# Half of nine weight splits per layer moved from GpSimd to VectorE, and one addition of squares moved into PSUM

## The chip, the core and the metric

The kernel runs on one core of a Trainium2 chip. The metric is the device time of one execution in microseconds. Five engines work side by side, each through a queue of its own in a fixed order: TensorE (PE in the profile, with its weight loads as PEld), VectorE (DVE), ScalarE (ACT), GpSimd (POOL) and SyncE (SP), which here issues nearly all transfers.

## What is computed

Two layers of a hybrid trunk over 640 tokens (512 latent, 128 context), model width 1024. Cut to what matters here:

```python
def trunk_layer(x, cvec, lw, layer, ctx):
    sh1, sc1, g1, sh2, sc2, g2 = modulation(cvec, lw['w_mod'], lw['b_mod'])
    h = rmsnorm(x, lw['g_mix']) * (1.0 + sc1) + sh1
    mixed, new_ctx = token_mixers(h, lw, layer, ctx)   # h @ w_in -> DA | MLA | NA | conv -> @ w_out
    x = x + g1 * mixed
    h = rmsnorm(x, lw['g_ff']) * (1.0 + sc2) + sh2
    x = x + g2 * (jnp.square(jax.nn.relu(h @ lw['w_ff1'])) @ lw['w_ff2'])
    return x, new_ctx
```

The columns of `h @ w_in` feed four groups: differential attention (DA), latent attention (MLA), neighbourhood attention (NA) and a convolution of 31 taps over 256 channels (conv). In MLA the low rank vectors are normalised first: `qm = heads(rmsnorm(mla_qd, lw['g_mla_q']) @ lw['w_mla_qup'], MLA_HEADS)`, where `mla_qd` has 256 columns.

## The kernel before

**Products from split numbers.** A large product is made of three matmuls (`mm3`, L245 to L247): each operand is split into a rounded high part and the rest, and high x high, high x low and low x high are summed in PSUM. Weights come in *granules* of 128 x 1024 floats, 94 per layer, in the order in which they are used. Granule n of the program (layer 1 begins at 94) is loaded into one of three raw buffers (`w_dma`, L215, on SP's queue), then split by `w_cut` in two halves of 512 columns: for each half ScalarE casts the high part (L193) and another engine subtracts to get the low part (L194). That engine is GpSimd, but for some halves that the condition in `w_cut` gives to VectorE. Of granules 4 to 29 of a layer ("mix" granules) the high and low parts alternate between two slots, so granule n can only be cast when TensorE is done with granule n-2, and the raw buffer of n takes granule n+3 when both halves are split.

**What granules 4 to 12 are.** 0 to 3 are the conv columns; 4 and 5 the NA values, 6 to 9 NA queries and keys (eight steps of 128 rows each, the second half of the granule being steps 4 to 7); 10 to 12 the DA values and the rotary key of MLA (three, three and two steps of 288 columns); 13 is the first of the DA queries, 14 of its keys.

**What else runs there.** When the conv columns are done, `conv_taps` puts 62 VectorE instructions on a background list (L420 and L424, two times 31 taps over 670 columns). They are traced with a lower priority than the work around them (`later`), and `conv_finish` begins with an addition of the two halves on GpSimd (L439) that needs the last of them. In layer 0 the modulation of that layer is computed in the same stretch (`mod_rows`): groups of four 512 KB tiles of `w_mod` are loaded by SP (L1363) into a ring of six, multiplied by TensorE (L1375), copied by ScalarE (L1382), gathered by TensorE (L1385) and added to the bias by VectorE (L1386).

**What sets the order.** The kernel's text gives each instruction a place and a priority; the framework's scheduler then fixes, when the program is built, the order of every engine's queue, by priority among what its own estimate of the times holds ready. On the chip a queue is not reordered: an instruction that waits holds all behind it.

**The low rank norm.** `lora_norm` (L630 to L646) squares each of its sources on ScalarE (L635), adds the two squares on GpSimd where there are two (L638), lets three steps of the surrounding work pass, sums over partitions by a matmul with a matrix of ones (L642), takes the inverse root (L338, L339) and scales. With two sources it is called twice per layer, for 384 and for 256 tokens; its three calls per layer for the key-value part have one source.

Of the kernel before, what the change touches and what calls it, by code (L numbers as in the profile page):

```python
# [12 lines left out]
ALU = mybir.AluOpType  # L13
# [18 lines left out]
NGRAN, NMIX = 94, 30  # L32
# [28 lines left out]
CUT = "DDDDDGDD"  # L61
# [22 lines left out]
class Builder:  # L84
# [133 lines left out]
    def w_cut(self):  # L218
        while self.w_split < min(self.w_load, self.ng):
            n = self.w_split  # L220
            i = self.w_slot(n)
            if self.held[i] or (i > 1 and self.we is None):
                return
            self.held[i] = True
            raw = self.w_raw(n)
            hi, lo = self.w_hl(n)
            for j, s in enumerate((slice(0, 512), slice(512, 1024))):
                self.split(hi[:, s], lo[:, s], raw[:, s], self.nc.vector if n < 4 and CUT[n * 2 + j] == "D" or n > 3 and j and i > 1 and n % NGRAN < NMIX + 4 else None)
            self.w_split += 1
            self.w_dma()  # L230

# [397 lines left out]
    def lora_norm(self, srcs, gains, scale):  # L629
        nc = self.nc  # L630
        n = srcs[0].shape[1]
        sqs = []
        for s in srcs:
            sq = self.tmp(n)
            nc.scalar.activation(sq, s, AF.Square)  # L635
            sqs.append(sq)
        if len(sqs) > 1:
            nc.gpsimd.tensor_tensor(out=sqs[0], in0=sqs[0], in1=sqs[1], op=ALU.add)  # L638
        for _ in range(3):
            yield  # L640
        ps = self.g()[:, 0:n]
        nc.tensor.matmul(ps, self.ones, sqs[0], start=True, stop=True)  # L642
        r = self.tmp(n)
        self.rsq(r, ps, scale)
        for s, g in zip(srcs, gains):
            nc.vector.scalar_tensor_tensor(out=s, in0=s, scalar=g, in1=r, op0=ALU.mult, op1=ALU.mult)  # L646
# [1067 lines left out]
```

## Time and profile before

| | us |
|---|---|
| median of 3 runs | 1711.4 (1711.36 to 1712.46) |
| profiled execution, its own time | 1712.74 |
| its span, first to last instruction | 1710.7 |
| TensorE busy | 1633.3 (95%) |
| VectorE busy | 1051.2 (61%) |
| ScalarE busy | 728.2 (43%) |
| GpSimd busy | 659.3 (39%) |

TensorE is nearly always at work, so its idle stretches, and the stretches in which its clock is granted at half, are what can be had. The waits are therefore read first, then the stretch around each of the long ones. All times inside the trace count from the first instruction.

### The profile page before, as it was taken

The page shows a single profiled execution, that of the slowest core. Times are in us where ns is not written, and L with a number is a line of the kernel's source. Part 1 is how long each engine was busy: PE and PEld are TensorE (multiplying, and loading weights), DVE is VectorE, ACT ScalarE, POOL GpSimd, SP SyncE. Part 2 cuts the span into 40 slices and gives each one's busy share as a digit, 9 for nine tenths or more (in the row PEclk, how much of TensorE's full clock was granted, in tenths as well). Part 3 has the DMA queues.
Part 4 walks back from the last instruction along what each step waited for, and adds up shares of the span by engine and source line. Part 5 has one row for each costly group of instructions (what it writes and reads, how often), then busy time and mean ns, then how long its engine had stood idle before and what let it go on. Part 6 is the DMA issues. An engine that isn't in the chain of part 4 may idle for free. (4 is left out here: it accounts for less than half of the span.)

```text
span 1710.7 us, 29286 instructions
## 1 busy us (share of the span) xinstructions
PE 1633.3 (95%) x11416; PEld 1531.2 (90%) x11416; DVE 1051.2 (61%) x2064; ACT 728.2 (43%) x1617; POOL 659.3 (39%) x527
## 2 busy tenths in 40 slices
PE   7989999999899999999999899999999999999997
PEld 4867988878899999999999888887789999999997
DVE  4791438867788787885377943886773333333335
ACT  4322576755622222233343257676553323332222
POOL 0242543414444444544324364341443333333330
PEclk7998999999999999999999999999999999999999
DMA  9465333302244454443222233330112222222221
GB/s 358 157 227 173 100 101 98 88 21 79 71 151 157 151 159 152 157 150 99 75 71 72 65 95 101 86 87 21 50 57 92 74 75 75 75 74 75 75 62 62
DMA packets 62330, 178.27 MB, mean 104 GB/s; under 512 B 8656, under 2 KB 20048, under 8 KB 62192
## 3 DMA queue, kind: packets, MB, share of 16 engines
q1 hardware_dynamic: 61984, 176.14, 33.7%
q8 instruction: 89, 1.46, 0.4%
q14 instruction: 49, 0.40, 0.1%
q0 software_dynamic: 64, 0.14, 0.0%
q10 hardware_dynamic: 144, 0.13, 0.0%
HBM read 158.52 MB, written 3.83 MB: 95 GB/s over the span
## 5 line engine op out<-in xcount | busy, mean ns | idle before, releaser
L194 POOL TENSOR_TENSOR ra<-fa,ra 128x512 fp32r<-128x512 f32 (+1 forms) x239 | 353.4, 1494 | 501.8 <-ACT ra L193 481.9
L194 POOL TENSOR_TENSOR we<-fa,we 128x512 fp32r<-128x512 f32 x126 | 185.7, 1485 | 261.3 <-ACT we L193 239.6
L1098 DVE TENSOR_TENSOR fr<-fr 128x384 f32<-128x384 f32 (+1 forms) x128 | 102.2, 800 | 281.5 <-ACT or L1097 153.5
L193 ACT CAST ra<-fa 128x512 fp32r<-128x512 f32 (+1 forms) x240 | 147.2, 622 | 252.7 <-PE s L246 152.7
L245 PE MATMUL s<-ra 128*128 128x256 f32 (+2 forms) x704 | 218.7, 311 | 2.4 <-DVE fa L1386 2.1
L246 PE MATMUL s<-ra 128*128 128x256 f32 (+2 forms) x704 | 217.8, 309 | 0.0
L247 PE MATMUL s<-ra 128*128 128x256 f32 (+2 forms) x704 | 217.4, 309 | 0.0
L393 DVE SCALAR_TENSOR_TENSOR fa<-s,fa 128x128 f32<-128x128 f32 (+1 forms) x312 | 121.9, 427 | 73.8 <-PE s L247 73.7
L193 ACT CAST we<-fa 128x512 fp32r<-128x512 f32 x132 | 81.5, 620 | 180.5 <-PE s L246 132.2
L302 DVE CUSTOM_DVE_ANT_0 fa<-fa 128x1024 f32<-128x1024 f32 x96 | 153.4, 1598 | 0.1
L245 PEld LDWEIGHTS s<-ra 128*128 128x128 f32 x704 | 134.2, 191 | 8.4 <-issue 4.0
L393 DVE SCALAR_TENSOR_TENSOR fa<-g,fa 128x128 f32<-128x128 f32 (+1 forms) x264 | 109.2, 443 | 44.5 <-PE g L247 43.8
L246 PEld LDWEIGHTS s<-ra 128*128 128x128 f32 x704 | 134.1, 190 | 2.4 <-issue 2.3
L247 PEld LDWEIGHTS s<-ra 128*128 128x128 f32 x704 | 134.0, 190 | 0.2 <-issue 0.2
L247 PE MATMUL g<-ra 128*128 128x256 f32 (+2 forms) x404 | 123.7, 306 | 9.1 <-POOL ra L194 9.1
L245 PE MATMUL g<-ra 128*128 128x256 f32 (+2 forms) x404 | 128.1, 317 | 0.7 <-ACT fa L656 0.4
L424 DVE SCALAR_TENSOR_TENSOR fa<-fa 128x670 f32<-128x670 f32 x120 | 127.0, 1123 | 0.4
L246 PE MATMUL g<-ra 128*128 128x256 f32 (+2 forms) x404 | 123.4, 306 | 0.0
L245 PE MATMUL g<-or,ra 128*128 128x384 f32 (+1 forms) x328 | 112.8, 344 | 4.8 <-DVE or L194 4.4
L246 PE MATMUL s<-ra,we 128*128 128x256 f32 (+1 forms) x360 | 112.2, 312 | 4.6 <-DVE ra L371 4.6
L245 PE MATMUL s<-ra,we 128*128 128x256 f32 (+1 forms) x360 | 110.6, 309 | 4.2 <-DVE fa L393 2.3
L247 PE MATMUL s<-ra,we 128*128 128x256 f32 (+1 forms) x360 | 110.5, 307 | 0.0
(294 smaller groups left out, 4425.1 us busy)
## 6 DMA issues: line engine op xcount, KB each, us to landing
fa<-in_wg SPq DMA_DIRECT2D x187, 512.0 KB, 3.7
fa<-in_wmod SPq DMA_DIRECT2D x68, 512.0 KB, 4.3
at<-in_wmod SPq DMA_DIRECT2D x25, 512.0 KB, 7.2
ra<-ra SPq DMA_DIRECT2D x64, 96.0 KB, 2.5
ra<-ra SPq DMA_DIRECT2D x64, 80.0 KB, 2.8
fa<-in_nab SPq DMA_DIRECT2D x24, 192.0 KB, 4.0
fa<-in_xT SPq DMA_DIRECT2D x8, 320.0 KB, 6.7
os<-in_wmod SPq DMA_DIRECT2D x3, 512.0 KB, 10.2
```

The source lines that it names most:

```text
L193: nc.scalar.copy(hi, src)
L194: (lo_eng or nc.gpsimd).tensor_tensor(out=lo, in0=src, in1=hi.bitcast(F32), op=ALU.subtract)
L245: nc.tensor.matmul(out, a[0], b[0], start=start, stop=False)
L246: nc.tensor.matmul(out, a[0], b[1], start=False, stop=False)
L247: nc.tensor.matmul(out, a[1], b[0], start=False, stop=stop)
L302: self.nc.vector.tensor_tensor_reduce(out=self.junk, in0=slot, in1=self.cb[:, v], scale=1.0, scalar=0.0, op0=ALU.mult, op1=ALU.add, accum_ ...
L393: self.mark = nc.vector.scalar_tensor_tensor(out=xs, in0=ps[:, a - t0:b - t0], scalar=self.mod(l, v, which)[:, m:m + 1], in1=xs, op0=ALU.m ...
L424: nc.vector.scalar_tensor_tensor(out=y, in0=g[:, j:j + 670], scalar=dwh[:, c, j:j + 1], in1=y, op0=ALU.mult, op1=ALU.add)
L1098: nc.vector.tensor_tensor(out=r, in0=r, in1=r, op=ALU.mult)
```

## The change

In `w_cut`, the second half (`j` is 1) of granules 4 to 12 of both layers is subtracted by VectorE instead of GpSimd; the first half stays on GpSimd. That is 18 instructions, 9 per layer. In `lora_norm`, the addition of the two squares on GpSimd is gone; the matmul with ones is done once per source and sums in PSUM, which makes one matmul more in each of the two calls per layer that have two sources.

```diff
-                self.split(hi[:, s], lo[:, s], raw[:, s], self.nc.vector if n < 4 and CUT[n * 2 + j] == "D" or n > 3 and j and i > 1 and n % NGRAN < NMIX + 4 else None)
+                self.split(hi[:, s], lo[:, s], raw[:, s], self.nc.vector if n < 4 and CUT[n * 2 + j] == "D" or n > 3 and j and (i > 1 and n % NGRAN < NMIX + 4 or 4 <= n % NGRAN < 13) else None)
```

```diff
             sqs.append(sq)
-        if len(sqs) > 1:
-            nc.gpsimd.tensor_tensor(out=sqs[0], in0=sqs[0], in1=sqs[1], op=ALU.add)
         for _ in range(3):
             yield
         ps = self.g()[:, 0:n]
-        nc.tensor.matmul(ps, self.ones, sqs[0], start=True, stop=True)
+        for sq in sqs:
+            nc.tensor.matmul(ps, self.ones, sq, start=sq is sqs[0], stop=sq is sqs[-1])
```

## Rows read from the trace of the kernel before

**Rows 1.** The page, busy time of engines: us, share, instructions.
```profile
PE 1633.3 (95%) x11416; PEld 1531.2 (90%) x11416; DVE 1051.2 (61%) x2064; ACT 728.2 (43%) x1617; POOL 659.3 (39%) x527
```
**Rows 2.** Waits of PE: engine, line, waited for: us in total, times, longest.
```profile
PE g L247 <- POOL ra L194: 9.1, 1, 9.1
PE s L1375 <- DMA at<-in_wmod: 5.8, 2, 4.4
...
PE s L245 <- DVE fa L1386: 2.1, 1, 2.1
...
PE g L642 <- POOL fa L638: 1.2, 2, 0.6
```
**Rows 3.** Timeline of PE, layer 1: start, length, instruction, idle before and releaser.
```profile
976.50 0.34 PE L246 MATMUL g<-ra 128*128 128x384 f32 x1
985.98 0.69 PE L247 MATMUL g<-ra 128*128 128x384 f32 x1 [9.14 <-POOL ra L194]
```
**Rows 4.** Timeline of POOL, layer 1.
```profile
964.75 3.73 POOL L194 TENSOR_TENSOR ra<-fa,ra 128x512 fp32r<-128x512 f32 x2 [3.29 <-ACT ra L193]
983.34 1.37 POOL L439 TENSOR_TENSOR fa<-fa 128x670 f32<-128x670 f32 x1 [14.86 <-DVE fa L424]
984.66 4.97 POOL L194 TENSOR_TENSOR ra<-fa,ra 128x512 fp32r<-128x512 f32 x4
```
**Rows 5.** Timeline of ACT, layer 1: second half of granule 105, then 106, 107.
```profile
958.37 0.62 ACT L193 CAST ra<-fa 128x512 fp32r<-128x512 f32 x1 [0.83 <-PE s L246]
...
964.05 1.15 ACT L193 CAST ra<-fa 128x512 fp32r<-128x512 f32 x2 [4.72 <-issue]
970.02 1.15 ACT L193 CAST ra<-fa 128x512 fp32r<-128x512 f32 x2 [4.82 <-issue]
```
**Rows 6.** Timeline of DVE, layer 1, and of its last 17 taps alone.
```profile
919.05 64.21 DVE L424 SCALAR_TENSOR_TENSOR fa<-fa 128x670 f32<-128x670 f32 x60
...
969.11 14.15 DVE L424 SCALAR_TENSOR_TENSOR fa<-fa 128x670 f32<-128x670 f32 x17
```
**Rows 7.** Line 194, 923 to 968.6 us: count, ns least, median, longest.
```profile
L194 POOL TENSOR_TENSOR ra<-fa,ra x14: 1290/1906/1985, 923.1 to 966.6; 128x512 fp32r<-128x512 f32 x14
```
**Rows 8.** Line 194, whole span, same columns.
```profile
L194 DVE TENSOR_TENSOR wes<-fa,wes x4: 684/684/686, 20.1 to 21.9; 128x512 fp32r<-128x512 f32 x4
```
**Rows 9.** Stretches at half clock: us, busy per engine, granted clock, DMA share, GB/s.
```profile
125.50:132.30 6.80, 5.89 (x27) 3.00 (x28) 6.62 (x11) 0.75 (x2) 0.00 (x0) 0.50 0.73 228
...
978.80:989.10 10.30, 3.12 (x10) 3.12 (x11) 7.47 (x18) 2.35 (x6) 5.76 (x5) 0.50 0.11 17
```
**Rows 10.** Timeline of PE, layer 0, products of the modulation.
```profile
112.03 1.46 PE L1375 MATMUL s<-at,fa 128*32 128x512 f32 x10
...
126.41 1.93 PE L1375 MATMUL s<-at,fa 128*32 128x512 f32 x8 [4.43 <-DMA at<-in_wmod]
```
**Rows 11.** Timeline of SP's issues, layer 0.
```profile
104.04 1.26 SPq L1363 DMA_DIRECT2D fa<-in_wmod  x2
116.44 0.33 SPq L215 DMA_DIRECT2D fa<-in_wg  x1
...
118.24 0.53 SPq L1363 DMA_DIRECT2D fa<-in_wmod  x1
```
**Rows 12.** Line 194, 104 to 120 us, columns as in rows 7.
```profile
L194 POOL TENSOR_TENSOR ra<-fa,ra x4: 1903/1908/8653, 105.9 to 118.2; 128x512 fp32r<-128x512 f32 x4
```
**Rows 13.** Timeline of PE around the first bias addition, layer 0.
```profile
89.13 1.04 PE L1375 MATMUL s<-fa 128*32 128x512 f32 x8
92.23 0.39 PE L245 MATMUL s<-ra 128*128 128x256 f32 x1 [2.06 <-DVE fa L1386]
```
**Rows 14.** Line 194 on POOL, 66 to 92 us, columns as in rows 7.
```profile
L194 POOL TENSOR_TENSOR ra<-fa,ra x6: 1325/1799/1902, 71.1 to 84.5; 128x512 fp32r<-128x512 f32 x6
```
**Rows 15.** Timeline of PE, sums of squares of the low rank norm, layer 0.
```profile
244.02 0.91 PE L642 MATMUL g<-fa 128*128 128x384 f32 x2
...
246.72 0.70 PE L642 MATMUL g<-fa 128*128 128x256 f32 x2 [0.59 <-POOL fa L638]
```

## The prediction

> **What bounds the kernel now.** Read the page first: TensorE is busy for 1633.3 us of a span of 1710.7 [rows 1]. Nothing is won by shortening other engines' work unless TensorE stops for it, so the view of TensorE's waits comes next [rows 2]. Four of its groups touch lines of this change: one wait of 9.1 us on a split by GpSimd, two of 5.8 us in total on transfers of the modulation's weights, one of 2.1 us on the bias addition L1386, and two of 0.6 us on the addition of squares that the change removes. The reader is to see that a single wait makes up the 9.1 us: splits on GpSimd are hundreds, and all but one of them are in time.
>
> **Where the 9.1 us come from.** TensorE stops at 976.84 and goes on at 985.98 [rows 3]; the low part that it needs is that of granule 107, the first after the nine that change. GpSimd was idle from 968.48 to 983.34, waiting for the last convolution tap of VectorE; its L439 stood ahead of four splits, and only then came those [rows 4]. Granule 107 had been cast at 970.02 to 971.17 [rows 5], so its split was held for some 13 us by the order of the queue alone. VectorE is the real limit: 60 taps without a pause from 919.05 to 983.26 [rows 6].
>
> Why do the taps take that long? The last 17, with GpSimd idle, take 14.15 us [rows 6], 0.83 each; sixty would take 49.8. They took 64.2. The surplus of 14.4 us lies over 14 splits on GpSimd [rows 7], 1.03 us each. The splits suffer too: 1.906 us in the middle, against 1.29 at best in the same stretch [rows 7]. A tap and a split on GpSimd thus hold each other up.
>
> The Trainium skill has this as a rule (SBUF — State Buffer, section "SBUF: two separate sides"): VectorE instructions with two SBUF inputs and GpSimd instructions take one pair of ports in turn, each for its whole length. The trace agrees in kind; by the rule alone a split would cost the taps its 1.29 us and not 1.03, and seven splits taken off would end them 1.8 us sooner than I say below. It also speaks against the change in part: the moved half has two SBUF inputs as well and can still collide with the half that stays.
>
> **Part 1, layer 1.** Seven granules (100 to 106) are split inside the taps, two splits each, which are the 14 of [rows 7]. Seven go to VectorE. Each takes 1.03 us of hindrance away and adds one VectorE split. Its price is 0.684 us in the only row of the like [rows 8]; the next starts 0.60 after it (four starts from 20.1 to 21.9), and I take 0.61 in a full queue. The queue of taps and splits so ends 7 x (1.03 - 0.61) = 2.9 us earlier, at 980.3. That alone brings TensorE back at 983.0.
>
> The larger effect is on the order. In the order as it was built, the last tap was held to be done before granule 107 was ready to be split, else the split would stand first. Now VectorE has seven to nine more instructions of 0.6 us ahead of its last tap, 4 to 5.5 us. The margin is not in the trace. With taps of 0.83 us and no hindrance, 60 of them from 919.05 would be planned to end at 968.9; granule 107 is ready at 970.6 to 971.2. The margin would be about 2 us, less than 4. I therefore expect L439 to slip behind the splits of 107, and GpSimd, free since 968, to make them at about 971 to 974, before TensorE asks at 976.8. The stop of 9.14 us goes, and with it the restart: from 978.8 to 989.1 the granted clock is 0.50 (1.2 GHz), with 3.12 us of TensorE work in it [rows 9], of which half, 1.6, is lost. Together 10.7.
>
> New waits come in return. The moved splits stand in VectorE's queue among taps, and that queue runs late on the chip by what was not planned: about 1.03 us for each of the splits that stay on GpSimd, six to seven by granules 105 and 106. Granule 105's second half is cast by 958.99, and TensorE starts on 105 when it leaves 104, when the cast of 106 begins, at 964.05; the second half is needed some 0.5 us in [rows 5]. That leaves 5 us less 0.66 for the split. For 106 (cast by 965.2, TensorE there at 970.0) it is as much. A lag of 6 to 7 makes waits of 1 to 1.5 us at each: 2.7 together. Bounds: 0 if the planned taps were longer than real ones, and at the other end the whole 10.7 if VectorE reaches 106 only at the end of the taps. Part 1: -10.7 + 2.7 = **-8.0**.
>
> **Part 2, layer 0.** Here TensorE waits for transfers, and the cause lies in SP's queue. SP issues nothing from 105.3 to 116.44: the load of granule 11 (L215) waits until the raw buffer of granule 8 is split [rows 11]. On GpSimd the first half of granule 8 took 8.653 us, shut out by taps, and the second only then had its turn [rows 12]. Behind it in SP's queue stand the loads for the modulation, issued from 118.24 on although TensorE had left their buffers at 113.5 [rows 10, 11]. They land for a start of TensorE at 126.41 instead of 121.97: 4.43 us. After it comes a stretch at clock 0.50 with 5.89 us of TensorE work [rows 9], 2.9 us lost.
>
> After the change the two halves of granule 8 are made by two engines side by side, and VectorE does not shut itself out. A GpSimd split that waits for one tap takes 1.9, so both halves should be done by about 110, before 113.5. The loads are then bound by TensorE, 4.7 us earlier; with the 8.2 us from issue to use they are there at 121.7. I count 4.43 + 2.9 = 7.3, less 2 that the next groups give back, since their loads follow each other closer: -5.3. Bounds: 0 and -7.3.
>
> The wait of 2.06 us on L1386 [rows 13] is VectorE's lag again: TensorE had its products done at 90.17 and waited for the bias addition, which stood behind taps. Six GpSimd splits lie ahead of it, granules 4 to 6 [rows 14]; with three of them it comes 3 x 1.03 = 3 us earlier, as moved splits displace taps behind it. -2.1. Bounds 0 and -2.1. In layer 0 L439 holds nobody up, and later VectorE ends of the taps cost nothing there, as no wait in the list names what follows [rows 2].
>
> **Part 3, the norm.** Two matmuls more per layer, one of 384 and one of 256 columns, each issued as two instructions: 0.91 and 0.70 us [rows 15], 3.2 us in both layers at most. The 1.2 us of waiting go, since the first square can be summed while ScalarE still makes the second. GpSimd saves four instructions that nobody else waits for. Between -1.2 (all hidden in the old gap) and +2.0; I take **+0.8**.
>
> **Sum.** -8.0 - 5.3 - 2.1 + 0.8 = -14.6. The profiled execution had 1712.74 us, 2.0 of them outside its span and 1.3 above the median; the difference is taken from the median: 1711.4 - 14.6 = 1696.8, so 1697.
>
> **Rivals.**
> *The order holds.* If L439 stays ahead of 107, TensorE resumes at 983.0 and layer 1 gives 2.9 and not 8.0: 1702. For it: the margin was inferred, not read. Against it: 4 to 5.5 us of added VectorE work.
> *SP is held all the same.* The one long split of 8.653 us shows that GpSimd can be shut out for eight taps, and a moved half that stands late in VectorE's queue holds the raw buffer as long. Then layer 0 gives only 2.1: 1702. With both rivals at once 1707.
> *VectorE's queue becomes the bound (slower).* If taps were planned much shorter than 0.83 us, the moved halves stand too far back and TensorE stops at most of the nine granules. It decides at a lag of about 5 to 7 us, the time between a cast and its use in [rows 5]. Five such stops of 2 us, each with a restart at half clock of the size seen in [rows 9] (1.6 to 2.9 lost, 2.2 in the middle), cost 21 against the 14.6 gained: 1718. Against it: in layer 1 all that VectorE must do ends earlier than before, so the stops before 976.8 largely replace the one after it.
> *It does not do what it says,* or both waits came from elsewhere: the second halves were not what TensorE waited for, only the queue behind L439 was. That is the first rival with the second, down to no change.
>
> **Chances.** Forecast 0.45, order holds 0.17, SP held 0.15, both 0.11, slower 0.12. About 0.2% (3.4 us) is what a measurement here can tell from no change: faster 0.78, same 0.10, slower 0.12. The range goes from 1690 (no new waits, nothing given back: -10.7 - 7.3 - 2.1 - 1.2) to 1709 and leaves out the slower case and a part of the one above it.
>
> **What would show it.** Right: GpSimd's splits of 107 before L439 in its queue, no wait of TensorE near 977, taps of layer 1 done some 3 us earlier, SP issuing the loads of L1363 near 114, no half clock after 121, no wait on L1386 near 90. Wrong: waits of TensorE on VectorE's L194 at several granules, GpSimd idle before L439 with splits behind it, another split of many us on GpSimd.

## The result, and the profile after

The changed kernel takes 1689.6 us in the median (1687.5 to 1690.7, 4 runs) against 1711.4 for the kernel before (4 runs). The ratio is 0.987 with an interval of 0.986 to 0.989: 21.8 us less. Put beside the kernel before a second time, in another series, it took 1690.35 us (6 runs), ratio 0.989 (0.987 to 0.991). The prediction was 1697.0 with 1690 as its low end. So the sign and two of the three places were right, and the gain was a third to a half larger than the 14.4 us forecast.

The profiled execution took 1689.8 us, its span is 1688.0. From line 638 on, a line of the changed kernel has a number one lower than before: L1375, L1386 and L642 are now L1374, L1385 and L641. The page's busy times (us, share, instructions), beside [rows 1]:

```profile
PE 1626.5 (96%) x11424; PEld 1526.6 (90%) x11424; DVE 1051.7 (62%) x2082; ACT 727.5 (43%) x1617; POOL 624.9 (37%) x505
```

TensorE has eight matmuls more and is busy for 6.8 us less, because less of its work lies in stretches at half clock (the mean granted clock is 0.991, before 0.984; one of the stretches is at the start of the program, below). VectorE has gained 18 instructions and hardly any busy time: what the splits added, the taps lost in hindrance.

**Layer 1.** TensorE's timeline (start, length, instruction, idle before it and releaser), beside [rows 3]:

```profile
952.34 0.40 PE L246 MATMUL s<-ra 128*128 128x288 f32 x1 [1.19 <-DVE ra L194]
959.76 0.40 PE L246 MATMUL s<-ra 128*128 128x288 f32 x1 [1.19 <-DVE ra L194]
972.61 0.94 PE L781 MATMUL s<-bt 64*128 64x128 f32 x12
974.58 0.41 PE L245 MATMUL g<-ra 128*128 128x384 f32 x1 [1.03 <-DVE bt L490]
```

The stop of 9.14 us has become three: two on second halves that VectorE makes (granules 105 and 106), and one of 1.03 us on something that the prediction does not name, the rotary step L490, which reads TensorE's last products of granule 107 out of PSUM. GpSimd in the same stretch, beside [rows 4]:

```profile
950.99 2.43 POOL L194 TENSOR_TENSOR ra<-fa,ra 128x512 fp32r<-128x512 f32 x1 [5.00 <-ACT ra L193]
958.42 4.28 POOL L194 TENSOR_TENSOR ra<-fa,ra 128x512 fp32r<-128x512 f32 x2 [5.00 <-ACT ra L193]
968.97 1.37 POOL L439 TENSOR_TENSOR fa<-fa 128x670 f32<-128x670 f32 x1 [6.26 <-DVE fa L424]
970.29 2.54 POOL L194 TENSOR_TENSOR ra<-fa,ra 128x512 fp32r<-128x512 f32 x2
```

Behind L439 there are two splits now, those of granule 108, and not four: the splits of 107 slipped ahead of it. VectorE in the same stretch, beside [rows 6]:

```profile
951.60 0.68 DVE L194 TENSOR_TENSOR ra<-fa,ra 128x512 fp32r<-128x512 f32 x1
952.21 6.89 DVE L424 SCALAR_TENSOR_TENSOR fa<-fa 128x670 f32<-128x670 f32 x7
959.02 0.68 DVE L194 TENSOR_TENSOR ra<-fa,ra 128x512 fp32r<-128x512 f32 x1
959.62 9.27 DVE L424 SCALAR_TENSOR_TENSOR fa<-fa 128x670 f32<-128x670 f32 x8
```

The last tap ends at 959.62 + 9.27 = 968.89, and the taps began at 905.13: 63.8 us, as against 64.2. In that time there were nine splits on GpSimd and seven on VectorE, sixteen instead of fourteen [rows 7].

**Layer 0.** The waits of TensorE from 60 to 150 us (us in total, times, longest), beside [rows 10, 13]:

```profile
PE s L1374 <- DMA fa<-in_wmod: 2.1, 1, 2.1
PE g L246 <- DVE ra L194: 1.1, 1, 1.1
PE s L1374 <- DVE fa L1385: 0.9, 1, 0.9
```

GpSimd's splits there, in the timeline, beside [rows 12]:

```profile
81.18 3.63 POOL L194 TENSOR_TENSOR ra<-fa,ra 128x512 fp32r<-128x512 f32 x1 [9.30 <-ACT ra L193]
91.21 3.58 POOL L194 TENSOR_TENSOR ra<-fa,ra 128x512 fp32r<-128x512 f32 x1 [6.40 <-PE s L247]
100.25 1.50 POOL L194 TENSOR_TENSOR ra<-fa,ra 128x512 fp32r<-128x512 f32 x1 [5.45 <-ACT ra L193]
```

SP's issues there, in the timeline, beside [rows 11]:

```profile
104.78 0.33 SPq L215 DMA_DIRECT2D fa<-in_wg  x1
...
107.00 0.34 SPq L1362 DMA_DIRECT2D fa<-in_wmod  x1
107.90 1.28 SPq L1362 DMA_DIRECT2D at<-in_wmod  x3
```

No split is held for 8.65 us any more, the load of granule 11 no longer blocks SP, and the modulation's loads go out at 107 instead of 118.24 (the changed kernel is 5.6 us ahead here, so 112.6 on the clock of before). The waits of 4.43, 2.06 and 1.39 us are gone. The half clock of [rows 9] is gone too. The stretches (us; busy time of the engines; granted clock; DMA share; GB/s) show 1.00 where 0.50 stood, and one short stretch at 0.50 behind the wait of 2.1 us:

```profile
122.00:132.00 10.00, 10.00 (x77) 8.55 (x75) 8.29 (x11) 2.71 (x6) 2.05 (x3) 1.00 0.78 277
135.30:138.70 3.40, 3.40 (x11) 1.80 (x8) 0.00 (x0) 0.00 (x0) 0.00 (x0) 0.50 0.64 229
965.00:975.00 10.00, 8.97 (x68) 8.55 (x67) 7.71 (x20) 3.33 (x10) 5.88 (x6) 1.00 0.20 62
```

**The norm.** The two sums of squares in layer 0, and the product that waits longest behind them, beside [rows 15]:

```profile
230.99 1.56 PE L641 MATMUL g<-fa 128*128 128x384 f32 x4
...
233.68 1.13 PE L641 MATMUL g<-fa 128*128 128x256 f32 x4
...
238.97 0.44 PE L245 MATMUL g<-or,ra 128*128 128x384 f32 x1 [1.11 <-DVE or L194]
```

That product does not use the normed vectors: `or` is an attention output that VectorE splits (L194).

**Where the time went.** The same instruction is looked up in both traces, and the difference of its start times says how far the changed kernel is ahead.

| instruction | before | after | ahead by |
|---|---|---|---|
| first split on GpSimd, layer 0 | 71.09 | 67.71 | 3.4 |
| first sum of squares, layer 0 | 244.02 | 230.99 | 13.0 |
| first product behind the norm, layer 0 | 253.29 | 238.97 | 14.3 |
| first tap, layer 1 | 919.05 | 905.13 | 13.9 |
| first sum of squares, layer 1 | 1056.92 | 1036.35 | 20.6 |
| first product behind the norm, layer 1 | 1066.20 | 1044.26 | 21.9 |
| end of the span | 1710.7 | 1688.0 | 22.7 |

So between these two traces layer 0 gave 9.6 us, layer 1's convolution 6.7, the norms 1.3 and 1.4, and a half-clock stretch behind the second norm (1067.6 to 1071.0 before, not there after) about 1.4 more; 0.4 was lost between the layers and 0.7 at the end. The 3.4 us at the start lie ahead of the first edited instruction and are no gain of the change: in the trace of before the early half clock lasted from 19.7 to 40.1 us, and in all the other traces of this study 10.2 or 13.7 us. Some 3 of the 9.6 us in layer 0 are no gain either: from the first split on GpSimd to the first sum of squares the trace of before took 172.9 us, but the five other kernels below that leave all of layer 0's splits as they were took 169.2 to 170.5, and the changed kernel 163.3. The second stretch at half clock of before, 146.0 to 152.8, is in none of the five.

### The profile page after: what moved, and what is told of

It reads as the page before. It is cut to its first block, busy times and chain, and to the rows that moved or that the text cites. A ratio compares the mean times of both kernels' runs of the same rounds, so it can differ in the third digit from the quotient of the medians.

```text
span 1688.0 us, 29280 instructions
## 1 busy us (share of the span) xinstructions
PE 1626.5 (96%) x11424; PEld 1526.6 (90%) x11424; DVE 1051.7 (62%) x2082; ACT 727.5 (43%) x1617; POOL 624.9 (37%) x505
## 5 line engine op out<-in xcount | busy, mean ns | idle before, releaser
L194 POOL TENSOR_TENSOR ra<-fa,ra 128x512 fp32r<-128x512 f32 x221 | 322.6, 1472 | 538.5 <-ACT ra L193 522.2
L194 POOL TENSOR_TENSOR we<-fa,we 128x512 fp32r<-128x512 f32 x126 | 185.5, 1484 | 261.4 <-ACT we L193 239.7
L424 DVE SCALAR_TENSOR_TENSOR fa<-fa 128x670 f32<-128x670 f32 x120 | 118.1, 1037 | 0.6
## 6 DMA issues: line engine op xcount, KB each, us to landing
os<-in_wmod SPq DMA_DIRECT2D x3, 512.0 KB, 10.2
```

Source lines behind the costliest of these rows:

```text
L194: (lo_eng or nc.gpsimd).tensor_tensor(out=lo, in0=src, in1=hi.bitcast(F32), op=ALU.subtract)
L424: nc.vector.scalar_tensor_tensor(out=y, in0=g[:, j:j + 670], scalar=dwh[:, c, j:j + 1], in1=y, op0=ALU.mult, op1=ALU.add)
```

## The experiments

Theory: the order on GpSimd's queue (L439 ahead of the splits of 107) costs the 9.14 us of layer 1, the held raw buffer costs the 4.43 us of layer 0, and the norm is worth next to nothing. Rival: VectorE is the bound behind both waits, and what the order gives back is taken by the next instruction that needs VectorE.

Times are medians; "before" is the kernel before on the same chip in the same series. Its single executions spread from 1702.5 to 1716.9 us in these series, its medians from 1708.5 to 1710.1, so the ratio and its interval are what counts.

The edits of the splits are all in the condition of `w_cut` that hands a half to VectorE; only that part of the line is shown.

**One part alone: the splits, without the norm.**

```diff
-j and i > 1 and n % NGRAN < NMIX + 4
+j and (i > 1 and n % NGRAN < NMIX + 4 or 4 <= n % NGRAN < 13)
```

> The split of granules 4 to 12 alone; the norm adds its squares on GpSimd as before. Theory (two waits of TensorE and their restarts at half clock are what was won, one behind GpSimd's queue in layer 1 and one behind SP's queue in layer 0): 15 to 19 us below the kernel before, no wait of TensorE above 3 us after the first 30 us, and the half clock at 1067 of before still there. Rival (a good part of the 21.8 us comes from the norm or from chance in the first 60 us): 9 to 13 us below.

Measured: 1693.4, ratio 0.991 (0.988 to 0.993), about 15.6 us less. That is the low end of what the theory had expected and leaves 3 to 6 us for the norm. The half clock behind the second norm is still there, as expected (1050.0 to 1053.5); one wait above 3 us is left after the first 30 us, of 3.3 at L354, far from the edits.

**One part alone: the norm.**

```diff
-        if len(sqs) > 1:
-            nc.gpsimd.tensor_tensor(out=sqs[0], in0=sqs[0], in1=sqs[1], op=ALU.add)
-        nc.tensor.matmul(ps, self.ones, sqs[0], start=True, stop=True)
+        for sq in sqs:
+            nc.tensor.matmul(ps, self.ones, sq, start=sq is sqs[0], stop=sq is sqs[-1])
```

> The squares summed in PSUM alone; all splits as before. By the sum on record: 0.8 us slower (from 1.2 faster to 2.0 slower). By the two traces laid side by side, in which the changed kernel gains 2.6 us between the rotary key and the end of the low rank norm of layer 1, where the half clock of 1067 to 1071 is gone: 2 to 3 us faster. The 9.1 us wait of layer 1 and the 4.4 us wait of layer 0 stay in both.

Measured: 1705.6 (12 runs), ratio 0.998 (0.996 to 0.9997): about 3.2 us less, not 0.8 more. VectorE's timeline in the kernel before, layer 0, and then TensorE's product that waits for it:

```profile
251.41 0.57 DVE L789 CUSTOM_DVE_ANT_0 s<-s,fa 128x384 f32<-128x384 f32 x1 [3.26 <-DMA fa<-in_nab]
...
251.90 0.88 DVE L646 SCALAR_TENSOR_TENSOR fa<-fa 128x256 f32<-128x256 f32 x2
...
252.95 0.28 DVE L194 TENSOR_TENSOR or<-g,or 128x128 fp32r<-128x128 f32 x1
...
253.29 0.44 PE L245 MATMUL g<-or,ra 128*128 128x384 f32 x1 [2.20 <-DVE or L194]
```

The same in this kernel (its lines are numbered one lower):

```profile
243.69 0.88 DVE L645 SCALAR_TENSOR_TENSOR fa<-fa 128x256 f32<-128x256 f32 x2 [0.44 <-ACT fa L339]
245.56 0.57 DVE L788 CUSTOM_DVE_ANT_0 s<-s,fa 128x384 f32<-128x384 f32 x1 [0.99 <-DMA fa<-in_nab]
...
246.05 0.28 DVE L194 TENSOR_TENSOR or<-g,or 128x128 fp32r<-128x128 f32 x1
...
246.39 0.45 PE L245 MATMUL g<-or,ra 128*128 128x384 f32 x1 [1.18 <-DVE or L194]
```

From the first sum of squares (238.34) to this product it is 8.05 us here; before it was 253.29 - 244.02 = 9.27. TensorE does more in that stretch and still gets through it 1.2 us sooner, because the wait ahead of the product has shrunk from 2.20 to 1.18 and the one on the addition (0.59) is gone. The cause of the larger part stands in VectorE's queue. L789 waits there for the load of a neighbourhood bias, `in_nab`. Before, the norm's two scalings (L646) and two short steps stood behind it and ahead of the split for the product; now the scalings (L645) stand ahead of it and fill idle time. The norm itself is not sooner: its second inverse root ends 5.25 us after the first sum of squares here and 5.14 before. In layer 1 the order has changed in the same way, it is 7.95 us against 9.28, and the half clock behind it has gone. The two waits are 1.9 to 2.4 us in all eight traces with the norm as before and 1.0 to 1.3 in all six with it changed. The half clock is less regular: it is missing in one of the eight and present in two of the six, both of the kernel with all halves on VectorE.

**One layer alone.** First layer 0, then layer 1:

```diff
-j and i > 1 and n % NGRAN < NMIX + 4
+j and (i > 1 and n % NGRAN < NMIX + 4 or 4 <= n < 13)
```

> The split moved in layer 0 alone (granules 4 to 12 of the program), norm as before. Theory: SP's queue is freed, the wait of 4.4 us with its half clock, the 2.1 us wait on the bias addition and perhaps the 1.4 us one go: 8 to 11 us faster; layer 1 keeps its 9.1 us wait. Rival (the one long split of GpSimd was the cause and comes again somewhere): 2 to 5 us faster.

Measured: 1699.6, ratio 0.995 (0.993 to 0.997), about 9.1 us less. The waits of 4.43 and 2.06 us are gone; that of 1.39 stays (1.38 at 87.81), and the stop of 9.14 in layer 1 is untouched. So the 1.39 us that the changed kernel also lost are not clearly the splits' doing.

```diff
-j and i > 1 and n % NGRAN < NMIX + 4
+j and (i > 1 and n % NGRAN < NMIX + 4 or NGRAN + 4 <= n < NGRAN + 13)
```

> The split moved in layer 1 alone (granules 98 to 106), norm as before. Theory: the splits of granule 107 stand before the sum of the convolution, the 9.1 us wait goes, two or three waits of about 1 us on VectorE's splits come: 6 to 9 us faster. Rival (GpSimd's order alone does not matter, only the taps end earlier): 3 us faster.

Measured: 1700.35, ratio 0.995 (0.994 to 0.997), about 8.4 us less. The waits in layer 1 are the three of the changed kernel (1.19, 1.19, 1.03); those of layer 0 stay. The three ratios of the norm, layer 0 and layer 1 multiply to 0.988, about 20.6 us: within the intervals the parts add up.

**The order alone.** L439 is taken out of GpSimd's queue, and nothing else is changed:

```diff
-        nc.gpsimd.tensor_tensor(out=ys, in0=y[0], in1=y[1], op=ALU.add)
+        nc.vector.tensor_tensor(out=ys, in0=y[0], in1=y[1], op=ALU.add)
```

> The kernel before, all splits as they were, but the sum of the two convolution halves (L439) is made by VectorE, behind its last tap, and so stands in no queue of GpSimd. Theory (the 9.1 us wait is GpSimd's queue held by L439, and nothing of VectorE's speed): the wait of TensorE in layer 1 is gone although the taps end as late as before (64 us for 60), 8 to 11 us faster; layer 0 keeps its 4.4 us wait. Rival (VectorE's load is what counts, so the splits had to move): the wait stays or comes back on another instruction behind the taps, less than 3 us faster.

Measured: 1710.3, ratio 1.001 (0.9997 to 1.003): nothing gained. The theory of the prediction falls here. TensorE's timeline in this kernel:

```profile
981.40 0.94 PE L782 MATMUL s<-bt 64*128 64x128 f32 x12
991.94 0.66 PE L245 MATMUL g<-ra 128*128 128x384 f32 x1 [9.60 <-DVE bt L490]
```

VectorE's timeline up to that restart:

```profile
985.40 0.86 DVE L439 TENSOR_TENSOR fa<-fa 128x670 f32<-128x670 f32 x1
...
987.91 0.57 DVE L789 CUSTOM_DVE_ANT_0 s<-s,fa 128x384 f32<-128x384 f32 x1
...
991.25 0.54 DVE L490 TENSOR_TENSOR bt<-g,fa 128x384 f32<-128x384 f32 x1
```

GpSimd's last four splits ahead of both, in the timeline:

```profile
968.67 3.15 POOL L194 TENSOR_TENSOR ra<-fa,ra 128x512 fp32r<-128x512 f32 x2 [2.26 <-ACT ra L193]
973.37 3.83 POOL L194 TENSOR_TENSOR ra<-fa,ra 128x512 fp32r<-128x512 f32 x2 [1.54 <-ACT ra L193]
```

The order did what was expected: the four splits are done by 977.2 and TensorE passes the old stop. It then runs for some 8 us and stops for 9.60 on the rotary step L490 of granule 107's columns. That step, with steps of the attention (L789, L722) ahead of it, stands in VectorE's queue behind the last tap. Moving L439 made it worse by 0.86 us for the addition and by four splits that now run beside taps: the taps took 68.4 us instead of 64.2.

This gives a new theory: once GpSimd's order is mended, layer 1's wait is set by the end of VectorE's last tap (or sum), and TensorE restarts a fixed time after it. Here that is 991.94 - 986.26 = 5.68 us. In the changed kernel it is 974.58 - 968.89 = 5.69.

**Fewer granules.** Instead of nine granules of layer 1, four (98 to 101) and six (98 to 103); each was run once:

```diff
-j and i > 1 and n % NGRAN < NMIX + 4
+j and (i > 1 and n % NGRAN < NMIX + 4 or NGRAN + 4 <= n < NGRAN + 8)
```

```diff
-j and i > 1 and n % NGRAN < NMIX + 4
+j and (i > 1 and n % NGRAN < NMIX + 4 or NGRAN + 4 <= n < NGRAN + 10)
```

> Layer 1 alone, second halves of four granules (98 to 101) moved, norm as before. In this build the sum of the convolution still stands ahead of all four splits of granules 107 and 108. Theory of the order: TensorE still waits for granule 107, and only as much less as the taps end earlier, 4 x 0.42 = 1.7 us at most: a wait of 7.4 to 9.2 us. Rival (the gain goes with the number of moved splits): 4 of 9, so a wait of about 5 us.

> As the last, but six granules (98 to 103). In this build both splits of granule 107 stand ahead of the sum. Theory of the order: the wait on granule 107 is gone (under 1 us). Rival (gain with the number): 6 of 9, so a wait of about 3 us.

The waits of TensorE from 930 to 1000 us (us in total, times, longest), with four granules:

```profile
PE g L247 <- POOL ra L194: 8.3, 1, 8.3
```

The same view with six:

```profile
PE g L245 <- DVE bt L490: 5.1, 1, 5.1
```

With four the splits of 107 still stand behind L439, and the stop has its old place, as the order theory says. With six they stand ahead of it, and the stop moves to L490. VectorE's last taps with six, in the timeline:

```profile
974.52 6.83 DVE L424 SCALAR_TENSOR_TENSOR fa<-fa 128x670 f32<-128x670 f32 x8
```

TensorE's restart with six, in the timeline:

```profile
987.04 0.66 PE L245 MATMUL g<-ra 128*128 128x384 f32 x1 [5.12 <-DVE bt L490]
```

987.04 - (974.52 + 6.83) = 5.69 us again. Neither side had the size of that wait (under 1 and 3 expected). The single times were 1707.3 and 1705.7, against a median of 1709.1 for before in the same series; both lie inside the spread of before.

**The changed kernel with L439 moved as well.** The new theory was tried against the old one with the edit of the order alone, now on top of the change.

> The changed kernel with the sum of the taps (L439) on VectorE instead of GpSimd. Theory, as it stands after the run with the sum alone moved: what TensorE waits for behind the convolution is the rotary step and the norm that stand behind the last tap in VectorE's queue, so what counts is when the last tap ends. Moving the sum puts 0.83 us more into that queue and lets the two splits of granule 108 run beside taps, at 1.03 us each: the wait of 1.03 us before the matmul that follows the twelve of L781 grows to about 3.9 us, and the time is about 3 us above the changed kernel. Rival, the theory of the prediction: the sum only held GpSimd's queue, so the time stays as the changed kernel's or falls by up to 1 us.

Measured: 1694.4, ratio 0.992 (0.990 to 0.994), beside 1690.35 for the changed kernel in the same series: 4.1 us more. TensorE's waits from 930 to 1000 us:

```profile
PE g L245 <- DVE bt L490: 3.7, 1, 3.7
```

VectorE's last steps, in the timeline:

```profile
969.84 0.92 DVE L424 SCALAR_TENSOR_TENSOR fa<-fa 128x670 f32<-128x670 f32 x1
970.80 0.86 DVE L439 TENSOR_TENSOR fa<-fa 128x670 f32<-128x670 f32 x1
```

The wait is 3.73 us (3.9 expected by the new theory, 1 or less by the old one), and TensorE restarts at 977.35, 5.69 us after the end of L439. The new theory holds here. The wait is 2.7 us longer than in the changed kernel, and behind it the clock is granted at half from 975.5 to 982.3, where the changed kernel has it at full. The intervals of the two ratios just overlap, but the trace says the same as the medians: an edit that freed a queue made the kernel slower.

**The held raw buffer alone.** Only the second half of granule 8 of layer 0 is moved:

```diff
-j and i > 1 and n % NGRAN < NMIX + 4
+j and (i > 1 and n % NGRAN < NMIX + 4 or n == 8)
```

> The kernel before with one single split moved: the second half of granule 8 of layer 0, from GpSimd to VectorE. Theory of part 2: the raw buffer of granule 8, held by the 8.65 us split and the one behind it, is what holds SP and so the loads of the modulation; with its two halves side by side SP issues the loads of L1362/L1363 from about 114 on, the wait of 4.4 us on the products of the modulation near 126 and the half clock before it go, and the time falls by 4 to 7 us. Rival: the first half on GpSimd is shut out by the taps all the same, or the load waits for something else; then the wait near 126 stays at 4 us or more and the time is within 2 us of the kernel before.

Measured: 1707.85, ratio 0.9987 (0.997 to 1.0003): 0.7 us less in the medians, and by the interval between 5.0 less and 0.5 more. GpSimd's split of granule 8, in the timeline:

```profile
104.24 4.97 POOL L194 TENSOR_TENSOR ra<-fa,ra 128x512 fp32r<-128x512 f32 x1 [5.85 <-ACT ra L193]
```

SP's issues behind it:

```profile
109.24 0.33 SPq L215 DMA_DIRECT2D fa<-in_wg  x1
...
111.03 0.55 SPq L1363 DMA_DIRECT2D fa<-in_wmod  x1
```

TensorE where the transfers were late before:

```profile
123.78 0.73 PE L1375 MATMUL s<-at,fa 128*32 128x512 f32 x4 [2.87 <-DVE fa L1386]
```

The mechanism is as predicted: SP's load of granule 11 goes out at 109.24, right behind the end of the split at 109.21, the modulation's loads follow at 111.03 (112.7 on the clock of before) instead of 118.24, and no wait on a transfer is left at that place. The gain falls short of the 4 to 7 us expected: TensorE waits there for the bias addition L1386 instead, which stands behind eleven taps. From the first split on GpSimd to the first sum of squares this trace took 167.4 us, 1.7 to 3.1 less than the five other traces with layer 0 as before. It is the pattern of layer 1 once more. With the halves of all nine granules moved, as in the run with layer 0 alone, no such wait is left; numbers between one and nine were not tried in layer 0.

**All of both halves on VectorE.** The condition on `j` is dropped for granules 4 to 12, so that GpSimd splits none of them:

```diff
-j and (i > 1 and n % NGRAN < NMIX + 4 or 4 <= n % NGRAN < 13)
+(j and i > 1 and n % NGRAN < NMIX + 4 or 4 <= n % NGRAN < 13)
```

> The changed kernel with both halves of granules 4 to 12 on VectorE, so that GpSimd makes no split while the taps run. Theory (what is left in the changed kernel, waits of 1.1 to 1.2 us on VectorE's splits, is the lag that GpSimd's remaining splits put on VectorE's queue, 1.03 us each): taps alone take 0.83 us each without exception, the waits on L194 go to under 0.5 us, and the time is 2 to 5 us below the changed kernel, some 25 below the kernel before. Rival (VectorE's queue is full and the lag comes from its own length): the waits on L194 grow, since the first halves are needed 2 us earlier than the second ones; slower than the changed kernel by 2 to 8 us.

> The changed kernel once more, beside the two others: ratio to the kernel before 0.986 to 0.990, some 1688 to 1692 us.

> Both halves of granules 4 to 12 on VectorE once more, now beside the changed kernel on the same chip. If its traces are right (in layer 1 one wait of 2.0 us in the place of 1.19, 1.19 and 1.03; in layer 0 the waits of 1.07 and 0.93 gone), it is 3 to 4 us below the changed kernel. Rival: the two ratios to the kernel before that were measured so far, 0.9873 and 0.9868, are the truth and it is level within 1 us.

Measured: 1685.4 (ratio 0.987, 0.984 to 0.990) in the first series; in the second 1686.06 (1685.6 to 1689.4, 5 runs; ratio 0.987, 0.986 to 0.989) beside 1690.35 (1687.7 to 1691.6, 6 runs) for the changed kernel. So it is 4.3 us faster in the medians; the two ratios to before overlap, so this is less sure than the gain over before. TensorE's waits in the second execution from 890 to 1000 us:

```profile
PE g L245 <- DVE fa L721: 2.0, 1, 2.0
```

The same view from 66 to 150 us:

```profile
PE s L1374 <- DMA fa<-in_wmod: 0.6, 1, 0.6
PE s L1374 <- DMA at<-in_wmod: 0.2, 1, 0.2
```

In layer 1 2.0 us of waiting stand against 3.4, in layer 0 0.8 (2.5 in the first execution) against 4.4 in the changed kernel's trace of the same series (2.4, 1.1 and 0.9). No half that VectorE makes is late here, although it makes twice as many.

Something else has changed with it, in VectorE's timeline of layer 1:

```profile
949.79 12.13 DVE L424 SCALAR_TENSOR_TENSOR fa<-fa 128x670 f32<-128x670 f32 x9
...
963.59 0.57 DVE L788 CUSTOM_DVE_ANT_0 s<-s,fa 128x384 f32<-128x384 f32 x1
...
965.98 0.89 DVE L424 SCALAR_TENSOR_TENSOR fa<-fa 128x670 f32<-128x670 f32 x1
```

Two rotary steps and the first step of the attention (L788) now stand ahead of the last two taps, and TensorE restarts at 967.97, 1.10 us after the last tap and not 5.69; it is 1.10 in the first execution too. So the fixed time belongs to the order of VectorE's queue and not to the taps, and how much of the 4.3 us comes from that order and how much from the splits is not shown. GpSimd still makes four splits beside taps, those of granules 107 and 108: the nine taps of the first line above took 12.13 us.

## Why the prediction was right and wrong

**What bounds the kernel.** Right on the place, half right on the cause. Its sentence "VectorE is the real limit" stands, and so does its price: with 18 splits beside the taps they took 68.36 us, (68.36 - 49.8) / 18 = 1.03 each, the figure taken from 14 of them [rows 6, 7]. The reading that all of GpSimd's splits but one are in time overlooks two waits of 0.7 us on splits of `or`, which changes nothing here. The step that failed is "its split was held for some 13 us by the order of the queue alone", read as if TensorE would run free once the order was mended. The prediction asked what is late next only for granules 105 and 106, not for what stands behind the last tap in VectorE's own queue. The rows had the end of the taps at 983.26 [rows 6]; 5.69 us later is 988.95. Without the 10.7 us of the old stop TensorE would have been there about 984.5 (the twelve matmuls of L782 begin at 994.26 in the trace of before and take 0.94), so some 4.4 us of the 9.14 could not be had by order at all. With the four splits beside taps and the moved addition on top (4 x 1.03 + 0.86) that makes 9.4, and 9.60 was measured.

**Part 1, layer 1: -8.0 predicted; -8.4 measured alone, -6.7 between the traces.** The two steps with numbers were right: L439 slipped behind the splits of 107, and the new waits on granules 105 and 106 came to 2.38 us for 2.7. The margin ("about 2 us, less than 4") is consistent with the order flipping between four and six moved granules. The missing term is the wait on L490. It came to no more than 1.03 us for two reasons: the taps ended a little earlier than they would have, though not by the 2.9 us of the prediction, since the two splits of 107 now ran beside them (2.9 - 2 x 1.03 = 0.8; the traces have 64.2 - 63.8 = 0.4); and TensorE itself arrived 2.4 us later because of the two waits ahead. 4.4 - 0.8 - 2.4 = 1.2. By this sum the two waits on 105 and 106 cost next to nothing: without them the same time would have been spent at L490. The -8.0 came out near the measured -8.4 although it lacks that wait, so part of the agreement is luck.

**Part 2, layer 0: -7.4 predicted; -9.1 measured alone (5.5 to 12.7 by the interval), -9.6 between the traces.** The chain raw buffer, SP, modulation's loads is shown by the run with granule 8 alone. What that run adds is that it was not enough by itself: VectorE's lag, which the prediction books only for the wait near 90 (2.1 us), also decides near 124, where 2.87 of the 4.43 us stay while L1386 is late. The size is borne out: against the five other traces with layer 0 as before (169.2 to 170.5 us for the stretch named above) the changed kernel's 163.3 is 5.9 to 7.2 less, and the rest of the 9.6 lies in the trace of before. New waits of 1.07 and 0.93 us came, for the "2 that the next groups give back". Both halves of granule 8 were done by 104.72 (VectorE's began at 104.04), 110.3 on the clock of before, where 110 was predicted.

**Part 3, the norm: +0.8 predicted, about -3.2 measured (0.5 to 6.2 less by the interval); the largest miss.** The failed step is the claim that two more matmuls cost their length, and that nothing but the 1.2 us of waiting on the addition goes. The reader of [rows 15] saw the wait on the addition, but not the wait of 2.20 us on a product behind it. Two things were wrong. The extra matmuls lengthen the sums by 0.65 and 0.43 us per layer (0.91 to 1.56, 0.70 to 1.13), 2.2 in both layers and not 3.2. And the wait of 2.20 shrank by 1.0 to 1.2 us in each layer, because with the edit VectorE's queue was built in another order, in which the norm's scalings no longer stand between the held L789 and the split that TensorE waits for. That the addition of 0.73 to 1.02 us on GpSimd is gone did not bring the norm's result sooner. So -1.2 was no bound: a term for the order of VectorE's queue is missing, and a stretch of half clock can go with the wait. That the scheduler would choose this order could not be seen in the rows, and why it did was not tried.

**The sum.** 14.4 predicted, 21.8 measured (18.8 in the second comparison). Of the 7 us between the first two numbers, 4 are the norm. The 1.7 by which layer 0 alone and the 0.4 by which layer 1 alone exceed their terms lie inside their intervals, and the kernel before, at 1711.4 in the first series, had medians of 1708.5 to 1710.1 in the others. The rest is not settled, and the spread of single executions does not let it be.

**The rivals.** "The order holds" did not happen; with four granules it did. "SP is held all the same" did not happen; its effect (little gained in layer 0) did, by way of L1386, when only granule 8 was moved. "VectorE's queue becomes the bound" was true as a mechanism, since the last wait of layer 1 is on VectorE in every kernel in which the order was mended, but in the changed kernel it costs 1.03 us; it took the whole gain only where L439 was moved instead of splits. The run with all halves on VectorE speaks against the fear behind it: with more splits on the queue none of them was late, though in that run the order of the queue had changed too.

**A rule beside it.** Beside taps, a split on GpSimd costs VectorE 1.03 us and one on VectorE itself 0.60 (from 959.02 to 959.62 above). The Trainium skill (SBUF — State Buffer, section "SBUF: two separate sides") has the port pair held for a whole instruction by whichever starts first. The trace agrees that they hold each other up, but they do not always take turns: single splits took 8.65, 4.97 or 3.6 us, and beside that of 8.65 (from 105.89 in the trace of before) VectorE ran eleven taps in 9.18 us from 104.23, 0.83 each, as if alone. Here a split can be shut out for several taps. The Trainium skill's advice that moving work between GpSimd and VectorE might not help, as they share that port (Perfetto Trace Analysis, section "Optimizing Scalar/DVE Operations"), is not borne out for the nine halves per layer (ratio 0.991 for the splits alone), and is for the sum L439, where moving it gained nothing (1.001).

## What to carry to other kernels

A wait that ends in an in-order queue has at least two causes, the order and the engine that the order waits for; before a gain is booked for mending one, look up what the waiting engine needs next and when that would be ready. An edit can be worth more, or less, at a wait that it does not touch: taking the addition out paid mostly through the new order of VectorE's queue, so the queues are to be read again after each build. Where VectorE's two-input work runs long beside GpSimd's, compare the price of the hindrance with that of doing the work on VectorE itself: here 1.03 against 0.60 us.

## What the runs showed that was not expected

- The time from the end of VectorE's convolution work to TensorE's restart was 5.68 to 5.70 us in six kernels in which the rotary steps and the attention's first steps stand behind the last tap, and 1.10 us in the one in which some of them stand ahead of the last two taps.
- One split on GpSimd beside back-to-back taps took 1.29, 1.9, 3.6, 4.97 or 8.65 us, for the same 128 x 512 elements. What decides between these was not tried.
- The half clock of TensorE early in the program lasted 20.4 us in one trace and 10.2 or 13.7 in the others, with the same instructions ahead of it. Later stretches at half clock (3.4 or 6.8 us) came and went between kernels at 240 to 250, 410 to 435 and 1050 to 1070 us, some of them where no edit was near; each is worth one to three us, about as much as the smaller edits here.
